# Layer 0 of a hybrid decoder step: convolution products of tile 3 ahead of the last tile 2 unit, tile 2's squares on two engines, the sample tile's squares in their own room

## The chip, the cores and the metric

The kernel runs on all 8 cores of one Trainium2 chip; every core works on one prompt sequence and on 16 of the 128 sample rows, with all the weights. The metric is the device time of the slowest core in microseconds (us). The fast runs of one kernel agreed within 0.2% here. Other runs were in a slower state, in which the cores of one or both dies were granted a lower TensorE clock: in the run of after that took 2964.3 us those of die 1 had 0.899 to 0.908 and those of die 0 0.998 to 0.999.

Engines: PE is TensorE, DVE is VectorE, ACT is ScalarE, POOL is GpSimd, SP is SyncE (here it issues DMA).

## The reference, cut to what matters

Four layers; the change is in the first third of layer 0 alone.

```python
def trunk(x, pool_prev, conv_prev, ffn_prev, pos0, p):
    for l in range(DEPTH):                        # 4
        h = rmsnorm(x, p['norm1'][l])             # D_MODEL 1024
        z = h @ p['w_in'][l]                      # one projection, 1792 columns
        za, zu, zv, zc = ...                      # A: pooling 256; B: u, v 384 each; C: 768
        a_out, pst = pool_mix(za, ...)            # trailing means over 2, 4, 8, 16 rows
        b_out = spatial_gate(zu, zv, ...)
        c_in = zc[..., :D_C] * jax.nn.sigmoid(zc[..., D_C:])     # "the product"
        c_conv, cst = causal_dwconv(c_in, conv_prev[l], ...)     # 31 taps, depthwise
        c_out = jax.nn.silu(layernorm(c_conv, ...))
        x = x + jnp.concatenate([a_out, b_out, c_out], axis=-1) @ p['w_out'][l]
        ...                                       # gated ConvFFN, 2 x 2816 columns
```

## The kernel before

Each core cuts its columns into tiles: 0 to 3 are 512 prompt positions each, 4 is the 64 sample positions. Layer 0 is written as a list of units, and the order of the list is the order of the instructions on each engine:

- `("sq", t)`: eight squares of tile t (one per 128 rows of x), for the RMSNorm; `"M"`: the matmuls with ones that add them up, followed by the reciprocal root on ACT; `("n", t, ks)`: normalised chunks of tile t on DVE.
- `("a", j, t)`: pooling projection j (two of them); its copy out of PSUM is on ACT. `("D", j, t)` and `("P", j, t)`: the pooling steps of (j, t), on DVE or on POOL.
- `("c", j, t)`: the two projections of convolution group j (three of them), the sigmoid on ACT, the product on DVE; for tiles 3 and 4 also a small copy of the new state ("staging").
- `("ho", j)`, `("hi", j)`: when all tiles of group j have their product it is written to DRAM and read back in another layout ("hop-out" and "hop-in"), from which PE makes the convolution as matmuls ("phase convolution").

```python
            def direct(self, ti, m, eng="act"):          # one square, and its sum matmul
                c0, n = TTS[ti]
                q = self.nb % 8                          # ring of eight square buffers, all tiles
                self.nb += 1
                sq = self.sqb[:, q, 0:n]
                src = X[:, m, c0:c0 + n]
                if eng == "act":
                    S.op("act", lambda e: e.activation(sq, src, AF.Square), reads=[RX[m][ti]], writes=[self.Rsq[q]])
                else:
                    S.op(eng, lambda e: e.tensor_tensor(sq, src, src, ALU.mult), reads=[RX[m][ti]], writes=[self.Rsq[q]])
                # ... def mm(): S.op("pe", matmul(pb, ONES, sq)) ... return mm
# ...
                        elif u == "M":
                            while sqs:
                                sqs.pop(0)()
# ...
                        elif u[0] == "sq":
                            sqs.extend(nrm.direct(u[1], m, "dve" if u[1] == 1 and m % 2 else "act") for m in range(KC))
# ...
                lo, hi = range(4), range(4, 8)
                run(("aa", 0, 0, 1), ("c", 0, 0), "T", ("sq", 1), ("c", 1, 0, ["M", ("n", 1, lo)]), ("n", 1, hi), ("P", 0, 0), "L", ("P", 1, 0),
                    ("sq", 4), ("aa", 1, 0), "M", ("sq", 2), ("n", 4, range(KC)), ("c", 0, 1, ["M", ("n", 2, lo)]), ("P", 0, 1), "B", ("c", 1, 1), ("sq", 3), ("n", 2, hi),
                    ("c", 2, 1), "T", ("a", 0, 2), "M", ("n", 3, lo), ("c", 0, 4), ("a", 0, 4), ("a", 1, 4), ("a", 1, 2), ("n", 3, hi), ("c", 1, 4), ("c", 0, 2), ("P", 0, 2), ("c", 1, 2), ("c", 2, 4), ("D", 0, 4),
                    ("c", 2, 2), ("D", 1, 4), ("c", 0, 3), ("ho", 0), ("hi", 0), ("D", 1, 1), ("P", 1, 2), ("c", 1, 3), ("ho", 1), ("c", 2, 3), ("ho", 2), ("hi", 1),
                    ("a", 0, 3), ("a", 1, 3), "O", ("hi", 2))
```

After this list come twelve phase convolutions, each evacuated by ACT and DVE, with the layer norm's sums ("statistics") between them, and then the v projection. The first matmul of the v projection is the mark that I use for the end of the changed part.

## Time and profile before

| | before |
|---|---|
| three runs, us | 2706.82, 2706.22, 3226.61 (slow state) |
| profiled run, us | 2708.28 (spans of the cores 2700.3 to 2707.2, mean 2704.56) |
| PE busy, slowest core | 2675.6 of 2707.2 us |
| first matmul of the v projection, core 5 / mean of 8 | 121.10 / 120.05 us |

The first line of the page and PE's line of its first part (busy us, share of the span, instructions), slowest core, which was core 5:

```profile
span 2707.2 us, 50040 instructions; the slowest of 8 cores (2700.3 to 2707.2 us)
PE 2675.6 (99%) x15858; PEld 1315.2 (49%) x15858; DVE 1745.4 (64%) x3001; ACT 1448.3 (53%) x2825; POOL 594.3 (22%) x898
```

PE is the bound; a gain can come only from time in which PE waits or runs slowly. PE's timeline on core 5. A row is start, duration, engine, line, operation, count, and in brackets the idle time before it with what ended it. L475 adds up squares, L591 is the projection, L886 the phase convolution:

```profile
43.32 3.62 PE L591 MATMUL ps<-H,wsall 128*128 128x512 bf16 x16
47.19 4.01 PE L475 MATMUL ps<-arena,ones 128*128 128x512 bf16 x8 [0.26 <-ACT arena L467]
51.04 8.17 PE L591 MATMUL ps<-H,wsall 128*128 128x512 bf16 x37
...
68.94 23.07 PE L591 MATMUL ps<-H,wsall 128*128 128x512 bf16 x120 [0.45 <-DVE arena L717]
93.12 0.27 PE L886 MATMUL ps<-arena 128*128 128x256 bf16 x1 [1.12 <-ACT arena L738]
...
103.52 0.34 PE L886 MATMUL ps<-arena 128*128 128x256 bf16 x1 [2.73 <-DMA arena<-hop]
```

Three things are to be seen. The eight sum matmuls at 47.19 take 4.01 us, against 1.9 us for eight such matmuls elsewhere (1.89 at 61.60 on this core). The first convolution waited 1.12 us, and the one at 103.52 waited 2.73 us for a hop-in. The squares of the slow group, ACT's timeline of core 5:

```profile
46.43 4.25 ACT L467 ACTIVATE arena<-X 128x512 bf16<-128x512 f32 x8
```

ACT makes all eight alone and starts late: in the list these squares stand behind other work of ACT (copies, a sigmoid, the sample tile's reciprocal root), since they reuse the eight buffers of the sample tile's squares. The issues of the hops, the timeline of SP on core 5 (`hop<-arena` is a hop-out, `arena<-hop` a hop-in):

```profile
85.37 0.33 SPq L138 DMA_DIRECT2D hop<-arena  x1
...
92.18 0.32 SPq L138 DMA_DIRECT2D hop<-arena  x1
...
93.88 0.32 SPq L138 DMA_DIRECT2D hop<-arena  x1
...
96.43 0.37 SPq L138 DMA_DIRECT2D arena<-hop  x1
```

What follows the 2.73 us wait is seen in the windows of core 5 (columns: window, its length, busy us of PE, PEld, DVE, ACT, POOL, then the granted clock, DMA share and GB/s):

```profile
core 5: us, PE busy (x) PEld busy (x) DVE busy (x) ACT busy (x) POOL busy (x), PEclk, DMA share, GB/s
104.00:108.00 4.00, 4.00 (x36) 3.00 (x35) 1.79 (x4) 1.63 (x4) 1.14 (x3) 0.63 1.01 158
```

PE is fully busy in 104 to 108, but at a granted clock of 0.63. DVE's timeline of core 5 at the end of the row that the order will change (L708 is a product, L911 the first evacuation on DVE):

```profile
90.97 1.07 DVE L708 TENSOR_TENSOR arena<-ps,arena 128x512 bf16<-128x512 f32 x1
...
92.68 1.07 DVE L708 TENSOR_TENSOR arena<-ps,arena 128x512 bf16<-128x512 f32 x1 [0.34 <-issue]
...
94.74 0.30 DVE L911 CAST arena<-arena 128x272 bf16<-128x272 f32 x1 [0.69 <-ACT arena L909]
```

### The profile page before, as it was taken

To read this page: it belongs to the slowest core of one execution; us is meant where nothing else is said; L and a number is where in the kernel's file an instruction comes from. 1 tells how busy PE (TensorE), PEld (TensorE's weight loads), DVE (VectorE), ACT (ScalarE), POOL (GpSimd) and SP (SyncE) were. 2 spreads that over 40 slices of the span, in tenths; PEclk is the share of its full clock that TensorE was granted. 3 is DMA by queue.
4 is the path that set the end of the run, shared out by engine and by line. 5 is a ranking of instruction groups with operands and counts; after the bars stand their busy time and mean duration, and the time that the engine had idled before them with its cause. 6 is when DMAs were issued, how large, how long until landed. Compare 5 with 4: busy or idle time off the path is not lost.

```text
span 2707.2 us, 50040 instructions; the slowest of 8 cores (2700.3 to 2707.2 us)
## 1 busy us (share of the span) xinstructions
PE 2675.6 (99%) x15858; PEld 1315.2 (49%) x15858; DVE 1745.4 (64%) x3001; ACT 1448.3 (53%) x2825; POOL 594.3 (22%) x898
## 2 busy tenths in 40 slices
PE   8999999999999999999999999999999999999998
PEld 3554444444465444444446444444445644444444
DVE  4758656566875765656686675565668677565566
ACT  5456627176364654627536473553753657273575
POOL 4444000003315200000412510000051350000005
PEclk9999999999999999999999999999999999999999
DMA  9643222125253321212426131212243522122113
GB/s 245 128 89 58 37 40 36 32 48 91 50 112 64 57 38 32 44 32 48 82 56 131 39 64 31 46 30 48 38 77 85 122 37 49 32 45 39 32 38 129
DMA packets 83888, 170.99 MB, mean 63 GB/s; under 512 B 11120, under 2 KB 44144, under 8 KB 83568
## 3 DMA queue, kind: packets, MB, share of 16 engines
q0 software_dynamic: 31568, 108.44, 24.3%
q1 hardware_dynamic: 52064, 59.35, 7.6%
q8 instruction: 134, 2.20, 0.3%
q14 instruction: 122, 1.00, 0.1%
HBM read 250.37 MB, written 28.39 MB: 103 GB/s over the span
## 4 chain that ended last, share of the span: by engine, by line
PE 92%; DVE 4%; DMA 1%; issue 1%; ACT 1%; SPq 1%; DVEq 0%; POOL 0%; ACTq 0%; POOLq 0%
PE ps L1192 23%; PE ps L1198 23%; PE ps L1108 17%; PE ps L1270 15%; PE ps L591 4%; PE ps L939 3%; PE ps L1036 3%; PE ps L886 1%; DVE arena L708 1%; PE ps L1022 1%; DVE arena L661 1%; DVE arena L645 1%; PE ps L860 1%; DMA X<-xt 1%; SPq L138 1%
## 5 line engine op out<-in xcount | busy, mean ns | idle before, releaser
L1192 PE MATMUL ps<-H,wsall 128*128 128x512 bf16 (+1 forms) x3520 | 700.2, 342 | 0.0
L1198 PE MATMUL ps<-H,wsall 128*128 128x512 bf16 (+1 forms) x3520 | 700.2, 342 | 0.0
L1212 DVE SCALAR_TENSOR_TENSOR arena<-arena,vt_s 128x512 f32<-128x512 f32 (+1 forms) x440 | 289.5, 658 | 382.7 <-ACT arena L1211 365.3
L1207 ACT COPY arena<-ps 128x512 f32<-128x512 f32 (+1 forms) x440 | 224.0, 509 | 576.2 <-PE ps L1192 576.2
L1108 PE MATMUL ps<-arena,wsall 128*128 128x512 bf16 (+2 forms) x2624 | 463.7, 338 | 1.9 <-issue 1.9
L1198 PEld LDWEIGHTS ps<-H,wsall 128*128 128x128 bf16 x3520 | 302.2, 98 | 332.2
L1192 PEld LDWEIGHTS ps<-H,wsall 128*128 128x128 bf16 x3520 | 302.1, 98 | 332.3
L1270 PE MATMUL ps<-arena,wsall 128*128 128x512 bf16 (+1 forms) x2240 | 401.1, 342 | 0.0
L1211 ACT ACTIVATE arena<-ps,vt_s 128x512 f32<-128x512 f32 (+1 forms) x440 | 309.4, 703 | 66.9 <-ACT arena L1207 4.4
L1108 PEld LDWEIGHTS ps<-arena,wsall 128*128 128x128 bf16 x2624 | 220.6, 98 | 237.0 <-issue 2.3
L418 POOL TENSOR_TENSOR arena<-arena 128x512 f32<-128x512 f32 (+2 forms) x273 | 293.7, 1076 | 157.0 <-ACT arena L412 126.2
L1214 DVE SCALAR_TENSOR_TENSOR arena<-arena,vt_s 128x512 f32<-128x512 f32 (+1 forms) x440 | 289.5, 658 | 47.5 <-DVE arena L1212 2.3
L1273 DVE TENSOR_TENSOR X<-ps,X 128x512 f32<-128x512 f32 (+1 forms) x320 | 184.6, 596 | 197.0 <-PE ps L1270 197.0
L412 ACT ACTIVATE arena<-X 128x512 f32<-128x512 f32 (+1 forms) x312 | 169.1, 552 | 239.4 <-DVE X L1110 197.0
L1270 PEld LDWEIGHTS ps<-arena,wsall 128*128 128x128 bf16 x2240 | 188.4, 98 | 211.4
L1110 DVE TENSOR_TENSOR X<-ps,X 128x512 f32<-128x512 f32 (+2 forms) x328 | 188.2, 585 | 142.0 <-PE ps L1108 131.1
L1225 DVE TENSOR_TENSOR arena<-arena 128x512 bf16<-128x512 bf16 (+1 forms) x440 | 260.6, 593 | 3.0 <-ACT arena L1224 2.7
L1217 ACT CAST arena<-ps 128x512 bf16<-128x512 f32 (+1 forms) x440 | 223.8, 509 | 56.2 <-PE ps L1198 48.7
L1224 ACT ACTIVATE arena<-arena 128x512 f32<-128x512 f32 (+1 forms) x440 | 245.4, 559 | 15.6 <-DVE arena L1214 14.9
L591 PE MATMUL ps<-H,wsall 128*128 128x512 bf16 (+1 forms) x1280 | 234.6, 343 | 6.4 <-DVE H L447 3.9
L1219 POOL COPY arena<-arena 128x2 f32<-128x2 f32 x88 | 18.3, 208 | 984.3 <-ACT arena L1207 984.3
L447 DVE SCALAR_TENSOR_TENSOR H<-X,vt_s,ps 128x512 bf16<-128x512 f32 (+1 forms) x320 | 207.2, 649 | 32.5 <-ACT ps L436 17.2
(117 smaller groups left out, 1866.7 us busy)
## 6 DMA issues: line engine op xcount, KB each, us to landing
wsall<-wup POOLq DMA_DIRECT2D x88, 512.0 KB, 6.2
arena<-bnd POOLq DMA_DIRECT2D x32, 480.0 KB, 14.7
wsall<-wdn POOLq DMA_DIRECT2D x32, 448.0 KB, 5.6
hop<-arena SPq DMA_DIRECT2D x24, 544.0 KB, 4.0
arena<-hop SPq DMA_DIRECT2D x24, 544.0 KB, 4.5
X<-xt SPq DMA_DIRECT2D x8, 1024.0 KB, 11.6
wsall<-wout POOLq DMA_DIRECT2D x16, 512.0 KB, 17.0
wsall<-wdn POOLq DMA_DIRECT2D x16, 512.0 KB, 6.2
```

Of the source, the lines that this page charges most:

```text
L418: S.op("pool", lambda e: e.tensor_tensor(dst, in0, sq, ALU.add), reads=R0 + Rs_, writes=Rd)
L591: S.op("pe", lambda e: e.matmul(pb[:, 0:n], wv[:, k, a:a + 128], H[:, k, c0:c0 + n], start=(k == 0), stop=(k == 7)), reads=[Rw, RH[k][ti]] ...
L1108: S.op("pe", lambda e: e.matmul(pb[:, 0:n], lh, rh, start=(q == 0), stop=(q == len(ops) - 1)), reads=rr, writes=[Rpb], inc=(q == len(ops) ...
L1192: S.op("pe", lambda e: e.matmul(pg[:, 0:n], wv[:, k, 0:128], H[:, k, c0:c0 + n], start=(k == 0), stop=(k == 7)), reads=[Rw, RH[k][ti]], wr ...
L1198: S.op("pe", lambda e: e.matmul(pv[:, 0:n], wv[:, k, 128:256], H[:, k, c0:c0 + n], start=(k == 0), stop=(k == 7)), reads=[Rw, RH[k][ti]], ...
L1207: S.op("act", lambda e: e.copy(G[:, gc:gc + n], pg[:, 0:n]), reads=[Rpg], writes=[gw_])
L1211: S.op("act", lambda e: e.activation(T_, pg[:, 0:n], AF.Identity, bias=fb, scale=w2), reads=[Rpg, Rvt2], writes=[Rtm[q]])
L1212: S.op("dve", lambda e: e.scalar_tensor_tensor(T_, G[:, gc - sh:gc - sh + n], w1, T_, ALU.mult, ALU.add), reads=gr_ + [Rvt2], writes=[Rtm[q]])
L1214: S.op("dve", lambda e: e.scalar_tensor_tensor(T_, G[:, gc - 2 * sh:gc - 2 * sh + n], w0, T_, ALU.mult, ALU.add), reads=gr_ + [Rvt2], writ ...
L1224: S.op("act", lambda e: e.activation(T_, T_, AF.Silu), reads=[Rtm[q]], writes=[Rtm[q]])
L1225: S.op("dve", lambda e: e.tensor_tensor(actb[:, fl, c0:c0 + n], VB_, T_, ALU.mult), reads=[Rvst[q], Rtm[q]], writes=[Rab[fl * 5 + ti]])
L1270: S.op("pe", lambda e: e.matmul(pb[:, 0:n], w[1][:, kk, m2 * 128:(m2 + 1) * 128], actb[:, kk, c0:c0 + n], start=(kk == 0), stop=(kk == nf ...
```

## The change

The intent: tile 2's squares early and on two engines, so that PE doesn't wait for them; and the products of groups 0 and 1 of tile 3 before group 2's tile 2, so that their hops leave early. No work is added. For it to be possible, the sample tile's squares get their own room, as the ring of eight buffers would otherwise tie tile 2's to them.

```diff
             def direct(self, ti, m, eng="act"):
                 c0, n = TTS[ti]
-                q = self.nb % 8
-                self.nb += 1
-                sq = self.sqb[:, q, 0:n]
+                if ti == 4 and self.small:
+                    sq, Rsq = self.ab[0][:, n * m:n * m + n], self.small[m]
+                else:
+                    q = self.nb % 8
+                    self.nb += 1
+                    sq, Rsq = self.sqb[:, q, 0:n], self.Rsq[q]
 ...
                         elif u == "M":
-                            while sqs:
+                            for _ in range(KC):
                                 sqs.pop(0)()
 ...
-                            sqs.extend(nrm.direct(u[1], m, "dve" if u[1] == 1 and m % 2 else "act") for m in range(KC))
+                            sqs.extend(nrm.direct(u[1], m, "dve" if u[1] == 1 and m % 2 or u[1] == 2 and m > 3 else "act") for m in range(KC))
 ...
-                    ("sq", 4), ("aa", 1, 0), "M", ("sq", 2), ("n", 4, range(KC)), ...
+                    ("sq", 4), ("sq", 2), ("aa", 1, 0), "M", ("n", 4, range(KC)), ...
-                    ..., ("c", 1, 2), ("c", 2, 4), ("D", 0, 4),
-                    ("c", 2, 2), ("D", 1, 4), ("c", 0, 3), ("ho", 0), ("hi", 0), ("D", 1, 1), ("P", 1, 2), ("c", 1, 3), ("ho", 1), ("c", 2, 3), ("ho", 2), ("hi", 1),
-                    ("a", 0, 3), ("a", 1, 3), "O", ("hi", 2))
+                    ..., ("c", 1, 2), ("c", 2, 4), ("c", 0, 3), ("ho", 0), ("hi", 0),
+                    ("D", 0, 4), ("c", 1, 3), ("ho", 1), ("hi", 1), ("D", 1, 4), ("P", 1, 2), ("c", 2, 2), ("D", 1, 1), ("c", 2, 3), ("ho", 2), ("a", 0, 3), ("a", 1, 3), "O", ("hi", 2))
```

More of the change, by code (lines that the diff above doesn't have):

```diff
@@ L398, in __init__ @@
                 self.nb = 0
+                self.small = None
                 self.gcol = gcol
@@ L461, in direct @@
                 c0, n = TTS[ti]
-                q = self.nb % 8
-                self.nb += 1
-                sq = self.sqb[:, q, 0:n]
+                if ti == 4 and self.small:
[4 more added lines that the diff above has]
+                    sq, Rsq = self.sqb[:, q, 0:n], self.Rsq[q]
                 src = X[:, m, c0:c0 + n]
                 if eng == "act":
-                    S.op("act", lambda e: e.activation(sq, src, AF.Square), reads=[RX[m][ti]], writes=[self.Rsq[q]])
+                    S.op("act", lambda e: e.activation(sq, src, AF.Square), reads=[RX[m][ti]], writes=[Rsq])
                 else:
-                    S.op(eng, lambda e: e.tensor_tensor(sq, src, src, ALU.mult), reads=[RX[m][ti]], writes=[self.Rsq[q]])
+                    S.op(eng, lambda e: e.tensor_tensor(sq, src, src, ALU.mult), reads=[RX[m][ti]], writes=[Rsq])
                 def mm():
@@ L475, in mm @@
                     S.op("pe", lambda e: e.matmul(pb[:, 0:n], ONES[:], sq, start=(m == 0), stop=(m == KC - 1)),
-                         reads=[self.Rsq[q], Rones], writes=[Rpb])
+                         reads=[Rsq, Rones], writes=[Rpb])
                     if m == KC - 1:
@@ L526, in build_nc @@
         nrm = Norm(NB, VT_N1)
+        nrm.small = AR.carve("sqs", NB, 256, 8)[1]
         tail = None
@@ L796, in build_nc @@
                 run(("aa", 0, 0, 1), ("c", 0, 0), "T", ("sq", 1), ("c", 1, 0, ["M", ("n", 1, lo)]), ("n", 1, hi), ("P", 0, 0), "L", ("P", 1, 0),
-                    ("sq", 4), ("aa", 1, 0), "M", ("sq", 2), ("n", 4, range(KC)), ("c", 0, 1, ["M", ("n", 2, lo)]), ("P", 0, 1), "B", ("c", 1, 1), ("sq", 3), ("n", 2, hi),
-                    ("c", 2, 1), "T", ("a", 0, 2), "M", ("n", 3, lo), ("c", 0, 4), ("a", 0, 4), ("a", 1, 4), ("a", 1, 2), ("n", 3, hi), ("c", 1, 4), ("c", 0, 2), ("P", 0, 2), ("c", 1, 2), ("c", 2, 4), ("D", 0, 4),
-                    ("c", 2, 2), ("D", 1, 4), ("c", 0, 3), ("ho", 0), ("hi", 0), ("D", 1, 1), ("P", 1, 2), ("c", 1, 3), ("ho", 1), ("c", 2, 3), ("ho", 2), ("hi", 1),
-                    ("a", 0, 3), ("a", 1, 3), "O", ("hi", 2))
+                    ("sq", 4), ("sq", 2), ("aa", 1, 0), "M", ("n", 4, range(KC)), ("c", 0, 1, ["M", ("n", 2, lo)]), ("P", 0, 1), "B", ("c", 1, 1), ("sq", 3), ("n", 2, hi),
+                    ("c", 2, 1), "T", ("a", 0, 2), "M", ("n", 3, lo), ("c", 0, 4), ("a", 0, 4), ("a", 1, 4), ("a", 1, 2), ("n", 3, hi), ("c", 1, 4), ("c", 0, 2), ("P", 0, 2), ("c", 1, 2), ("c", 2, 4), ("c", 0, 3), ("ho", 0), ("hi", 0),
+                    ("D", 0, 4), ("c", 1, 3), ("ho", 1), ("hi", 1), ("D", 1, 4), ("P", 1, 2), ("c", 2, 2), ("D", 1, 1), ("c", 2, 3), ("ho", 2), ("a", 0, 3), ("a", 1, 3), "O", ("hi", 2))
                 for j in range(2):
```

## The prediction

> **What bounds it now.** The tensor engine is busy 99% of 2707.2 us (page, part 1). The change touches layer 0 alone, the first 120 us. PE's losses there on the slowest core, core 5 (timeline of PE): (a) eight sum matmuls of tile 2's squares take 47.2 to 51.2, 4.0 us where eight cost 1.7: ACT alone makes the squares, 0.53 us each, from 46.4; (b) 1.4 us in three waits for tile 2's normalised chunks (DVE); (c) 1.1 us before the first phase convolution at 93.1 (hop-in 0 lands at 92.7); (d) 2.7 us at 103.5 for hop-in 1, issued at 96.4 behind hop-out 2, landed 103.4; (e) half-speed matmuls after it (pitch 0.24 instead of 0.13 us; granted clock 0.83 in 100:110). [...] From 121 us on PE hardly waits, so what layer 0 saves reaches the end.
>
> **What changes.** No work is added.
> 1. Tile 2's squares: four on ACT after X's first half lands (38.4), four on DVE (0.64 each, as tile 1's) after the second half (42.6), done about 45.2, before PE finishes the projection at 46.9. (a) shrinks to 1.7: PE gains 2.5 us. (b) stays: DVE still makes the same chunks between two products.
> 2. Tile 3's products of groups 0 and 1 come before group 2's tile 2. Hop-out 0 should issue near 77 (85.4 now), hop-out 1 near 80.5 (92.2), hop-in 1 near 85, landing near 90, needed at 98 to 101. (c) and (d) vanish.
> 3. But DVE then carries D04, product, D14 (4.9), product, D11 (5.6), product in one row. PE ends its projections near 89.4, DVE group 2's last product only near 92.7 (94.0 now). [...] the copy of a13 behind D11, and group 2's bank, hold up the second convolution: about 2 us of new PE waiting. The first evacuation starts 1.7 us sooner than now, not 3.6.
>
> **Sum on core 5:** 1.7 from the earlier start, 3.0 from (d) and (e): 4.7 us. Check: core 7 today has no hop stall (0.2 us) and needs 23.4 us from first evacuation to v projection, core 5 26.4; it ends at 2700.3. By the same count core 0 gains 4.3, core 1 5.0, core 7 0.8. The slowest core falls to about 2702; cores draw together.
>
> **Predicted time** 2702.0 us, eight in ten between 2699.3 and 2704.8. Faster by over 2% 0.01, within 2% 0.97, slower 0.02 (a slow-state median).
>
> **What would show it.** Step 1: tile 2's sum matmuls in about 1.8 us, DVE squares near 42.6 to 45.2, the first 64-wide group 2.6 us earlier. Step 2: hop-in 1 issued before hop-out 2, landing before 93; no wait of PE for a hop. Step 3: a new PE wait of 1.5 to 3 us near 89 to 93 released by DVE (or ACT's copy after D11); v projection near 116.4 on core 5 (121.1 now).
>
> **What would make it wrong.** DVE's pool steps may run at other speeds (POOL runs beside them: one op took 0.45 to 1.2 us), moving step 3 by 2 us either way. The new wait could drop the clock again, 1 to 2 us. Bands 6 and 7, asked for after the fourth convolution, take 8.5 to 11 us and could arrive late. X's halves could land after 43.9 on some core and hold DVE up. Chance waits later (1.9 us of issue and 0.8 us for a weight in layer 2 on core 5) decide which core is slowest.

The sum came to 1.7 + 3.0 = 4.7 us on core 5. The 2 us of new waiting in step 3 was my estimate.

## More of the kernel before

Hop-in 1 is issued only at 96.43. Hop-out 2 stands ahead of it in SP's order, but that is not what holds it: its turn comes when hop-out 1, issued at 92.18, has landed. The chain of work that ended last, core 5 (`--critical`: start, duration, what):

```profile
92.18 4.18 DMA hop<-arena
96.43 6.95 DMA arena<-hop
```

On all eight cores hop-in 1 was issued 0.06 to 0.07 us after hop-out 1 had landed, so what makes it late is group 1's product of tile 3.

## The result, and the profile after

| | before | after |
|---|---|---|
| runs, us | 2706.82, 2706.22, 2708.66, (3226.61 slow) | 2706.07, 2704.9, 2704.14, (2964.3 slow) |
| median of all runs, us | 2707.74 | 2705.49 |
| median of the fast runs, us | 2706.82 | 2704.90 |
| first matmul of the v projection, mean of 8 cores, us | 120.05 | 117.55 |
| mean span of the 8 cores, profiled run, us | 2704.56 | 2703.14 |
| slowest core, profiled run, us | 2707.2 (core 5) | 2705.0 (core 1) |

A ratio is the mean time of one kernel's fast runs over that of the other's fast runs of the same rounds, so not quite the ratio of the medians quoted. Here it is 0.9992, with a 95% interval of 0.9969 to 1.0015: the interval does not exclude that nothing was gained. The median of 2705.49 us lies 0.7 us above the range that I gave, that of the fast runs 0.1 us.

The page of after, its slowest core (core 1):

```profile
span 2705.0 us, 50045 instructions; the slowest of 8 cores (2701.3 to 2705.0 us)
PE 2675.8 (99%) x15858; PEld 1314.8 (49%) x15858; DVE 1748.5 (65%) x3005; ACT 1445.2 (53%) x2821; POOL 592.1 (22%) x898
```

PE's timeline on core 5, as before (L479 sums, L596 projection, L890 convolution, L864 statistics):

```profile
47.32 1.89 PE L479 MATMUL ps<-arena,ones 128*128 128x512 bf16 x8
...
66.94 23.07 PE L596 MATMUL ps<-H,wsall 128*128 128x512 bf16 x120 [0.44 <-DVE arena L722]
89.85 0.27 PE L890 MATMUL ps<-arena 128*128 128x256 bf16 x1
...
93.52 0.27 PE L890 MATMUL ps<-arena 128*128 128x256 bf16 x1 [1.53 <-DVE arena L722]
...
95.24 0.61 PE L864 MATMUL ps<-arena,oneb 128*128 128x272 bf16 x3 [0.73 <-DVE arena L918]
```

The sums at 47.32 take 1.89 us instead of 4.01, and no wait for a hop is left. In their place stand 1.53 us before the second convolution, released by DVE's L722, a staging copy, and 0.73 us before the second to fourth statistics matmuls (0.28 us at this place before), released by DVE's L918. All of PE's waits for that line at the statistics came to 2.6 us on core 5, against 1.2 before (`--waits`, 60 to 125 us). Now DVE's timeline of core 5 (L473 tile 2's squares, L713 products, L666 and L650 pooling steps, L722 staging, L915 evacuation):

```profile
42.37 3.61 DVE L473 TENSOR_TENSOR arena<-X 128x512 bf16<-128x512 f32 x4 [0.85 <-DMA X<-xt]
...
76.38 1.08 DVE L713 TENSOR_TENSOR arena<-ps,arena 128x512 bf16<-128x512 f32 x1 [2.38 <-PE ps L596]
...
77.67 1.18 DVE L666 TENSOR_TENSOR fb<-arena 128x291 f32<-128x291 f32 x1
...
91.34 0.75 DVE L650 SCALAR_TENSOR_TENSOR arena<-arena,cstt 128x512 bf16<-128x512 f32 x1
92.01 1.07 DVE L713 TENSOR_TENSOR arena<-ps,arena 128x512 bf16<-128x512 f32 x1
...
93.67 0.30 DVE L915 CAST arena<-arena 128x272 bf16<-128x272 f32 x1 [0.30 <-ACT arena L913]
```

DVE sat idle 2.38 us until the first product at 76.38, and then worked through products and pooling steps in one row until 93. ACT on core 5 (L471 squares, L617 the copy of the last pooling projection, L913 the first evacuation):

```profile
38.93 2.19 ACT L471 ACTIVATE arena<-X 128x512 bf16<-128x512 f32 x4 [1.94 <-DMA X<-xt]
...
92.18 0.20 ACT L617 COPY arena<-arena 128x15 f32<-128x15 f32 x1 [3.16 <-DVE arena L650]
...
93.09 0.48 ACT L913 ACTIVATE arena<-ps,cvq_s 128x272 f32<-128x272 f32 x1
```

ACT waited 3.16 us for DVE's pooling step D11 (L650, started at 91.34) before the copy at 92.18, and so made the first evacuation only at 93.09, though PE had begun the convolutions at 89.85. The hops, SP's timeline:

```profile
77.60 0.33 SPq L138 DMA_DIRECT2D hop<-arena  x1
...
82.26 0.32 SPq L138 DMA_DIRECT2D hop<-arena  x1
...
87.16 0.37 SPq L138 DMA_DIRECT2D arena<-hop  x1
93.21 0.32 SPq L138 DMA_DIRECT2D hop<-arena  x1
```

Hop-in 1 is issued at 87.16, 9.3 us sooner. On cores 2, 3, 6 and 7 the granted clock fell behind the new wait, as it had behind the hop's wait on core 5 of before; windows of core 3 of after:

```profile
97.00:100.00 3.00, 3.00 (x23) 2.09 (x21) 2.13 (x6) 1.43 (x4) 0.00 (x0) 0.50 0.40 81
```

PE is busy for 3.00 of 3.00 us at a granted clock of 0.50. On core 5 there was no such drop. In the traces' clock records each core's clock changes on a grid of 3.41 us: the drop lasted one such step on cores 2, 6 and 7 and two on core 3. In the step just before it PE was busy for 1.4 to 1.6 us on these four cores; the lowest steps of cores 0, 1, 4 and 5 at this place had 1.8 to 2.1 us, and no drop followed (`--windows`). Counted on this grid from 45 to 125 us in the traces of before and after, all nine drops followed a step in which PE was busy for 20 to 52% of the time; the lowest step with no drop behind it had 51%. More than this count is not shown.

### The profile page after: what moved, and what is told of

It reads as the page before. It is cut to its first block, busy times and chain, and to the rows that moved or that the text cites. A ratio compares the mean times of both kernels' runs of the same rounds, so it can differ in the third digit from the quotient of the medians.

```text
span 2705.0 us, 50045 instructions; the slowest of 8 cores (2701.3 to 2705.0 us)
## 1 busy us (share of the span) xinstructions
PE 2675.8 (99%) x15858; PEld 1314.8 (49%) x15858; DVE 1748.5 (65%) x3005; ACT 1445.2 (53%) x2821; POOL 592.1 (22%) x898
## 4 chain that ended last, share of the span: by engine, by line
PE 94%; DVE 3%; DMA 1%; issue 1%; ACT 1%; SPq 1%; POOL 0%; DVEq 0%; ACTq 0%; POOLq 0%
PE ps L1202 23%; PE ps L1196 23%; PE ps L1112 17%; PE ps L1274 15%; PE ps L596 6%; PE ps L943 3%; PE ps L1040 3%; PE ps L890 1%; PE ps L1026 1%; PE ps L864 1%; SPq L138 1%; DMA X<-win 1%; DMA wsall<-win 1%; DVE arena L713 0%; DVE H L448 0%
## 5 line engine op out<-in xcount | busy, mean ns | idle before, releaser
L596 PE MATMUL ps<-H,wsall 128*128 128x512 bf16 (+1 forms) x1280 | 234.7, 344 | 7.1 <-DVE H L448 4.1
```

The lines of the kernel that those rows point to most:

```text
L596: S.op("pe", lambda e: e.matmul(pb[:, 0:n], wv[:, k, a:a + 128], H[:, k, c0:c0 + n], start=(k == 0), stop=(k == 7)), reads=[Rw, RH[k][ti]] ...
```

## The experiments

My theory, A: the squares bring PE forward and earn what layer 0 gained; the order removes the hop waits, but DVE's row behind it ends no earlier, so that the time it saves turns into a wait for DVE and for ACT's copy. Its rivals are that the order earned the gain, or that both did in equal parts; and, for the new wait, D: it is caused by the pooling step D11 standing ahead of group 2's last product, and moving D11 away would give the time back. All twelve kernels compute what the reference computes, and all gave correct results.

The table gives the marks, in us. "Cores 4-7" is needed for squares, order, fill and late11, whose chip had die 0 throttled in every run (mean granted clock 0.984 to 0.998). In the trace of order that began only after 240 us, so its marks stand for all eight cores; in those of squares (cores 0 and 1), fill and late11 (cores 0 to 3) the clock was 0.81 for 15 us from about 47 to 48 us on, and on cores 6 and 7 of late11 for 4 us.

| kernel | tile 2's sums | first convolution | first DVE evacuation | v projection | v projection, cores 4-7 |
|---|---|---|---|---|---|
| before | 3.63 | 93.64 | 95.25 | 120.05 | 119.56 |
| after | 1.52 | 89.89 | 93.63 | 117.55 | 117.36 |
| again (repeat of after) | 1.51 | 89.77 | 93.64 | 117.35 | 117.03 |
| squares | 1.58 | 91.59 | 93.25 | 118.01 | 117.29 |
| order | 3.63 | 92.52 | 95.73 | 119.11 | 119.39 |
| fill | 1.57 | 90.14 | 92.76 | 116.19 | 115.77 |
| fill_again (repeat of fill) | 1.51 | 90.19 | 92.59 | 116.10 | 116.36 |
| late11 | 1.66 | 90.34 | 95.47 | 119.94 | 119.32 |
| fill_pad | 1.52 | 90.16 | 92.55 | 115.84 | 115.83 |
| before_spin27 (layer 0 as before) | 3.63 | 93.05 | 94.66 | 119.14 | 118.84 |
| before_dve8 (layer 0 as before) | 3.63 | 94.56 | 96.17 | 119.88 | 119.81 |
| spin23 (layer 0 as after) | 1.51 | 90.22 | 93.82 | 117.52 | 117.23 |

(A mark is the mean over cores; the sums are counted from the start of the first matmul to the start of the last, so 3.63 here is the 4.01 of the timeline. The last three rows show what a repeat is worth: a mean of before's layer 0 moves by 0.9 us from run to run, one of after's by 0.2. The cores of one run lie 2 to 8 us apart at this mark.)

### squares: the change of the squares alone

```diff
-  ("c", 2, 4), ("c", 0, 3), ("ho", 0), ("hi", 0), ("D", 0, 4), ("c", 1, 3), ("ho", 1), ("hi", 1), ("D", 1, 4), ...
+  ("c", 2, 4), ("D", 0, 4), ("c", 2, 2), ("D", 1, 4), ("c", 0, 3), ("ho", 0), ("hi", 0), ("D", 1, 1), ...      # as before
```

> The changed kernel with the unit order of before from tile 3 on; only the squares of tile 2 and the sample tile are changed. Theory A (the gain of the squares shifts everything after them, the vector engine's row behind it included): tile 2's eight sum matmuls take about 1.8 us instead of 4.0, every later mark of layer 0 comes 2.3 to 2.6 us sooner, the hop waits stay (PE waits of 1 to 4 us for the hop on most cores), the v projection starts 2.3 us sooner than before in the mean of the cores (about 117.8), time about 2705. Rival B (the squares' gain is swallowed by the hop and only the order counts): the v projection starts less than 0.7 us sooner than before.

On the undisturbed die the v projection came at 117.29, 2.3 us before that of before; its four cores lie far apart, though, from 114.55 to 123.02. The waits for the hops stayed: for hop-in 1 they were 0.40 to 2.75 us on the eight cores, in the mean 1.6, against 0.17 to 2.90 and 1.8 in before. PE's timeline of core 5, where that wait was 0.73 us instead of 2.73:

```profile
89.80 0.27 PE L891 MATMUL ps<-arena 128*128 128x256 bf16 x1 [0.85 <-ACT arena L743]
...
98.22 0.27 PE L891 MATMUL ps<-arena 128*128 128x256 bf16 x1 [0.73 <-DMA arena<-hop]
```

Five rounds: 1.0005 (0.9973 to 1.0037), on a chip with die 0 throttled; the mean span of cores 4 to 7 was 2703.65 us (6 runs) against 2705.33 (10 runs of before). So the squares alone give about what both parts together give at the v projection (117.29 against 117.36; different chips, and a spread that leaves 2 us open). The first evacuation, before the waits for hop-in 1, says the same: 93.25, against 94.7 to 96.2 in before and its two repeats, and 93.6 to 93.8 in after and its repeats.

### order: the change of the order alone

```diff
-  ("c", 2, 4), ("D", 0, 4), ("c", 2, 2), ("D", 1, 4), ("c", 0, 3), ("ho", 0), ("hi", 0), ("D", 1, 1), ("P", 1, 2), ("c", 1, 3), ("ho", 1), ...
+  ("c", 2, 4), ("c", 0, 3), ("ho", 0), ("hi", 0), ("D", 0, 4), ("c", 1, 3), ("ho", 1), ("hi", 1), ("D", 1, 4), ("P", 1, 2), ...     # as after
```

> The kernel before with the changed unit order from tile 3 on; the squares are as before. Theory A: the hop waits vanish, but the vector engine's row D04, product, D14, product, D11, product starts 2.5 us later than in the changed kernel and ends 2.5 us later, so the first evacuation comes at about 96 (94.7 before on core 5) and the v projection starts at about 120.0 in the mean of the cores, that is 0 to 0.5 us sooner than before: the order alone gains next to nothing, time 2706 to 2708. Rival B (the order does the work): the v projection starts 2 us or more sooner than before, time about 2705.

PE's timeline of core 5 of this kernel (L475 sums, L885 convolution):

```profile
49.70 4.01 PE L475 MATMUL ps<-arena,ones 128*128 128x512 bf16 x8 [0.25 <-ACT arena L467]
...
96.69 0.27 PE L885 MATMUL ps<-arena 128*128 128x256 bf16 x1 [0.23 <-DVE arena L717]
```

The sums take 4.01 us as before, and the second convolution waits 0.23 us; no core waits for a hop. But the first evacuation moved from 95.25 to 95.73 (DVE's row ends later). From there to the v projection it took 23.4 us instead of 24.8, so that the v projection came at 119.11 in the mean of eight cores, 0.9 us sooner than before; on cores 4 to 7 at 119.39, only 0.2 us sooner than before's 119.56 on another chip. A had expected 0 to 0.5 us, B 2 or more. Time: 0.9999 (0.9954 to 1.0045), three fast runs. At this mark little is gained: most of the wait removed was turned into others, on DVE's row and at the statistics (2.6 us on most cores, as in after).

The end of the program doesn't bear the split out: over the same rounds the mean span of cores 4 to 7 was 2703.63 us in order (3 undisturbed runs), as low as that of squares (2703.65) and 1.7 us under before's 2705.33. The standard error of that difference is about 0.6 us. So how much of the gain is the order's stays open between the 0.2 us of the mark and this; that the hop waits became other waits is what the traces show.

### late11: D11 after group 2's last product

```diff
-  ("D", 1, 4), ("P", 1, 2), ("c", 2, 2), ("D", 1, 1), ("c", 2, 3), ("ho", 2), ("a", 0, 3), ...
+  ("D", 1, 4), ("P", 1, 2), ("c", 2, 2), ("c", 2, 3), ("ho", 2), ("D", 1, 1), ("a", 0, 3), ...
```

> The changed kernel with D11 after group 2's last product and hop-out 2, still ahead of a13. Theory A (the scalar engine's copy of a13 behind D11 holds the first evacuation as much as the bank of group 2 holds the second convolution): the PE wait before the second convolution is gone, hop-out 2 issues about 5 us sooner (88), yet the first evacuation stays within 0.4 us of the changed kernel's (93.7 on core 5), because the copy still waits for D11; the v projection moves by less than 0.7 us. Rival D (the wait that the profile names, the bank of group 2, is the whole cost): the v projection comes 1.5 us or more sooner.

ACT's timeline of core 5 of this kernel:

```profile
94.09 0.20 ACT L617 COPY arena<-arena 128x15 f32<-128x15 f32 x1 [3.64 <-DVE arena L650]
...
95.00 0.48 ACT L913 ACTIVATE arena<-ps,cvq_s 128x272 f32<-128x272 f32 x1
```

And PE's, at the statistics:

```profile
96.21 0.28 PE L864 MATMUL ps<-arena,oneb 128*128 128x272 bf16 x1 [2.13 <-DVE arena L915]
```

The wait before the second convolution vanished, as D said. But the copy at 94.09 waited 3.64 us for D11, which now ended later, the first evacuation on ACT came at 95.00 (93.09 in after), PE waited 2.13 us at the statistics instead (2.1 to 3.6 us on the eight cores, and on seven of them the clock then fell to 0.50), and the v projection came 2.0 us later than after's on the undisturbed die. Rival D falls. Theory A had its direction (no gain) and not its size: I had expected 0.4 to 0.7 us of change, as I hadn't counted that D11 is pushed back by the product now ahead of it.

### fill: two pooling steps earlier, into DVE's idle time

```diff
-  ("c", 2, 4), ("c", 0, 3), ("ho", 0), ("hi", 0), ("D", 0, 4), ("c", 1, 3), ("ho", 1), ("hi", 1), ("D", 1, 4), ("P", 1, 2), ...
+  ("c", 2, 4), ("D", 0, 4), ("c", 0, 3), ("ho", 0), ("hi", 0), ("D", 1, 4), ("c", 1, 3), ("ho", 1), ("hi", 1), ("P", 1, 2), ...
```

> The changed kernel with D04 ahead of group 0's tile 3 product and D14 ahead of group 1's, so that the vector engine works through the 2.4 us in which it waits for that product; nothing else. Theory A (the length of the vector engine's row sets the start of the convolutions): group 2's last product ends near 90.7 to 91.5 instead of 93.1, the PE wait at the second convolution shrinks from 1.5 to under 0.5 us, the first evacuation comes 1.5 to 2.5 us sooner and so does the v projection (mean of the cores about 115.5), time 1.5 to 2.5 us under the changed kernel. Rival C (the evacuation waits for the hop or a13's copy and not for the row): unchanged within 0.5 us.

> The kernel with D04 ahead of group 0's and D14 ahead of group 1's tile 3 product, timed on the same chip as the changed kernel. Theory A: 1 to 2 us faster than the changed kernel, 3.5 to 5 us faster than the kernel before; v projection at about 116.0 in the mean of the cores. Rival: within 0.5 us of the changed kernel.

DVE's timeline of core 5, repeat run on an undisturbed chip:

```profile
74.05 0.45 DVE L666 TENSOR_TENSOR fb<-arena 128x291 f32<-128x291 f32 x1
...
91.02 1.07 DVE L713 TENSOR_TENSOR arena<-ps,arena 128x512 bf16<-128x512 f32 x1
...
92.68 0.30 DVE L915 CAST arena<-arena 128x272 bf16<-128x272 f32 x1 [0.29 <-ACT arena L913]
```

PE's, at the second convolution:

```profile
92.53 0.27 PE L890 MATMUL ps<-arena 128*128 128x256 bf16 x1 [0.41 <-DVE arena L722]
```

D04 now runs at 74.05, where DVE had idled; the last product starts at 91.02 instead of 92.01, the first evacuation at 92.68 instead of 93.67, and PE's wait falls from 1.53 to 0.41 us. The v projection came 1.6 us sooner on cores 4 to 7 in the first run and 1.25 us sooner than `again` in the mean of eight in the second: the direction and, at the low end, the size that A had expected. The first evacuation gained 1.05 us over `again`, less than the 1.5 to 2.5 expected. Time of the second: median 2704.13 us, 0.9988 (0.9976 to 1.0001); `again`, in the same rounds, 2705.56 us, 0.9992 (0.9979 to 1.0006). In the throttled rounds of the first run the interval (0.9979 to 1.0051) tells nothing; the undisturbed die had 2701.21 us (4 runs) against 2705.33 (10 runs of before).

### again, spin23, before_spin27: what comes after layer 0

In the mean, 2.5 us gained at the v projection had become 1.4 us at the end: from v projection to end of span a core took 2584.5 us before and 2585.6 after. I cut that stretch into stages, each bounded by the same two DVE instructions in every kernel (found by counting from the last one) and named by their times in before. Some stages differ between the two kernels by fixed amounts, equal on all eight cores to 0.03 us (one of them to 0.2). Theory T: PE's instruction stream is four records longer, and that shifts something. Two kernels change PE's stream by two matmuls of the warm-up.

```diff
 # spin23, against after
-        spin(25)
+        spin(23)
 # before_spin27, against before
-        spin(25)
+        spin(27)
```

> The changed kernel once more, as the reference on the same chip for the runs beside it and for a second set of eight core traces. Theory A: in the mean of the cores the v projection starts at 117.5 (before 120.05), 2.0 to 3.0 us sooner than before, and the time is 1.5 to 3 us under before, less than the 4.7 us forecast.

> The changed kernel with two of the 25 idle matmuls at its very start left out, so that the tensor engine's whole instruction stream after layer 0 stands four instructions earlier, where it stood in the kernel before (18556 records instead of 18560). Nothing else. Theory T (the 1.1 us that the changed kernel lost after layer 0, in the same places on all eight cores, comes from where its instructions stand in the stream): from v projection to the end it takes 2584.0 to 2584.9 us in the mean of the cores as before (2584.5) instead of 2585.6, and the gaps of 0.4 to 0.6 us at the 12025th, 12368th and 12434th matmul, present on all cores of the changed kernel and on hardly any before, are gone. Rival U (the loss comes from the other engines' streams or from the shifted timing): it stays at 2585.3 to 2586 with those gaps.

> The kernel before with two more idle matmuls at its start: its tensor stream then stands where the changed kernel's stands (18560 records). Theory T: from v projection to end 2585.2 to 2586 us instead of 2584.5, and the changed kernel's gaps at the 12025th, 12368th and 12434th matmul (two places later here) appear on all cores; the marks of layer 0 stay within a us of before. Rival U: the tail stays at 2584 to 2585 with the gaps of before.

The repeat gave 117.35 at the v projection, so layer 0's gain holds. The two spin kernels behaved as their parents in every fixed stage: the stage at 2100 to 2110 us took 11.08 us in before_spin27 as in before, 11.78 in spin23 as in after (11.82). Theory T falls. The whole stretch to the end would not have decided it: it took 2585.1 us in before_spin27 and 2585.2 in spin23, each between the values of the two theories (and 2585.9 in again). Times: 1.0003 (0.999 to 1.0015) for before_spin27 and 0.9991 (0.9979 to 1.0004) for spin23.

One other stage, at 1320 to 1330 us in layer 2, differs from core to core and run to run (10.7 to 13.2 us; in the page of before it is the 1.9 us of "issue" that PE lost on core 5 at L1108). Its mean was 11.42 in before, 12.07 in after, 12.18 in again, 11.51 in spin23, 11.67 in fill_again. It goes with no part of the change that I could name.

### all_act: tile 2's squares early, but all on ACT

```diff
-  "dve" if u[1] == 1 and m % 2 or u[1] == 2 and m > 3 else "act"
+  "dve" if u[1] == 1 and m % 2 else "act"
```

> The kernel after, with all eight squares of tile 2 on ACT again (in their new place ahead of the projection, the sample tile's squares in their own room). It splits the squares change into its two parts. If the place is what gains, ACT makes four squares after X's first half lands and four after the second (42.6 on core 5), 0.53 us each, done near 45, and the eight sum matmuls take 1.5 to 1.9 us as after: the v projection within 0.3 us of after's mean 117.4 to 117.6. If sharing between two engines is what gains, the sums take over 3 us and the v projection comes 1.5 to 2 us later. For what is lost again behind layer 0: DVE's and ACT's streams are nearly those of before, so the stage of layer 2 (2100 to 2110) that took 11.08 us before and 11.8 after on all cores should take 11.1 if it hangs on the length of the instruction streams of the elementwise engines, and 11.8 if not.

Neither expectation for layer 0 was met. ACT's timeline of core 5, the second four squares:

```profile
43.43 2.19 ACT L471 ACTIVATE arena<-X 128x512 bf16<-128x512 f32 x4 [2.45 <-DMA X<-xt]
```

DVE's, the first product behind them:

```profile
47.77 1.08 DVE L713 TENSOR_TENSOR arena<-ps,arena 128x512 bf16<-128x512 f32 x1 [6.29 <-ACT arena L710]
```

PE's, the sums and the last row of projections:

```profile
48.26 1.89 PE L479 MATMUL ps<-arena,ones 128*128 128x512 bf16 x8
...
70.34 1.89 PE L596 MATMUL ps<-H,wsall 128*128 128x512 bf16 x8 [0.44 <-DVE arena L722]
```

The sums take 1.89 us, so the early place is what shortens them. But the second half of x lands late, ACT waits for it (2.45 us) with its copies and sigmoids queued behind, DVE waits 6.29 us for ACT's sigmoid, and everything behind is late: the last row of projections starts at 70.34 (66.94 in after, 68.94 in before). The v projection came at 120.43 on cores 4 to 7, 0.9 us later than before; part of this is a granted clock of 0.50 for 3.4 to 6.8 us from about 61 us, on all four. Sharing the squares with DVE is what keeps ACT's queue moving: the early place on ACT alone doesn't pay. Sharing in the old, late place was not tested. Time: this run's profile fell in the slow state (die 0), so I use cores 4 to 7 alone, which ran at 0.996 to 0.997; two fast runs gave 0.9996 (0.9967 to 1.0025).

For the fixed stages it was decisive. With ACT's and DVE's streams as long as before's, each had before's value: 690 to 720 us took 30.48 on the undisturbed cores, 1450 to 1500 took 50.98, 1800 to 2090 took 290.41 and 2100 to 2110 took 11.08 on three of the four.

### before_dve8, after_act7: longer streams on the elementwise engines

```diff
 # before_dve8, against before
+  for _ in range(8):
+      S.op("dve", lambda e: e.memset(EPST[:, 1:2], 0.0), writes=[Rdum])
 # after_act7, against after
+  for _ in range(7):
+      S.op("act", lambda e: e.activation(EPST[:, 1:2], EPST[:, 0:1], AF.Square), reads=[Rones], writes=[Rdum])
```

> The kernel before with eight writes of one column on DVE at its start, so that DVE's stream is as long as after's (6252 records). Layer 0 as before (v projection 119 to 120 in the mean). If the place of DVE's instructions in their stream makes the fixed shifts of stages in layers 1 and 2, the stage 2100 to 2110 takes 11.8 us on all cores as after; if ACT's or nothing of the kind, 11.08.

> The kernel after with seven one-column squares on ACT at its start, so that ACT's stream is as long as before's (6721 records). Layer 0 as after (v projection 117.4 to 117.6 in the mean). If the place of ACT's instructions in their stream makes the fixed shifts, the stage 2100 to 2110 takes 11.1 us on all cores as before; otherwise 11.8.

Both paddings were longer than meant: each operation waits for the one before it, and a wait is a record of its own. They added 15 and 14 records, not 8 and 7. So the two expected values (11.8 and 11.1 in the stage at 2100) were not met: it was 11.08 and 11.34. The 11.08 is what the first expectation had named for the rival; as the stream was 7 records longer than meant, it decides nothing. But the stages moved, with nothing changed but the length of a stream:

| stage, us from the start | before | all_act | before_dve8 | after_act7 | after | fill_again | fill_pad |
|---|---|---|---|---|---|---|---|
| records DVE / ACT | 6244 / 6721 | 6244 / 6721 | 6259 / 6721 | 6252 / 6728 | 6252 / 6714 | 6251 / 6714 | 6259 / 6721 |
| 690-720 | 30.48 | 30.48 | 30.12 | 30.12 | 30.12 | 30.12 | 30.12 |
| 730-760 | 30.01 | 30.02 | 29.87 | 30.22 | 30.21 | 30.22 | 29.86 |
| 1450-1500 | 50.99 | 50.98 | 51.34 | 51.34 | 51.34 | 51.34 | 51.34 |
| 1800-2090 | 290.41 | 290.40 | 290.07 | 290.35 | 290.63 | 290.35 | 290.05 |
| 2100-2110 | 11.08 | 11.08 | 11.08 | 11.34 | 11.82 | 11.61 | 11.08 |
| 2600-2690 | 89.09 | - | 88.74 | - | 88.99 | 88.74 | 88.74 |

(Medians over unthrottled cores; for after in the stage at 2100 the mean, its cores lie between 11.71 and 11.87. In after_act7 both dies were throttled for parts of the run, at a mean granted clock of 0.953 to 0.967; its values are given for stages in which all its cores agree. Its time is not used.)

This led to the cause. I numbered all records of DVE in a trace from its first, semaphore waits included, and looked at the time from each record to the next. At nearly every record whose number leaves 59 when divided by 128 there is a pause: nine in ten of these gaps are over 0.32 us in every kernel (over 0.38 in before and after), while in any other residue the shortest tenth is about 0.07 us. ACT has the same at the same residue (the shortest tenth from 0.25 to 0.30 us), in every kernel, less sharply in after_act7 (0.09); POOL has one too (0.33 us at residue 64); PE's sequencer shows none. Since the pause falls on the same records on all eight cores (the shortest tenth at this residue is 0.39 us on each core of before and of after), moving it shows as a difference without scatter. Lining up before with before_dve8, where DVE's stream alone differs, nearly all steps of about 0.35 us in DVE's times (493 of 510 on the eight cores, 125 us to the end) lie within a few records of such a record of the one kernel or of the other; with after, where ACT's pauses have moved as well, 485 of 655 do. One of them, DVE's timeline on core 1 of before (L712 and L717 are the sample tile's product and its staging copy):

```profile
711.68 0.23 DVE L712 TENSOR_TENSOR arena<-ps,arena 128x64 bf16<-128x64 f32 x1 [3.53 <-ACT arena L705]
712.38 0.23 DVE L717 TENSOR_TENSOR arena<-ps,arena 128x64 f32<-128x64 f32 x1 [0.47 <-DVE arena L712]
```

The same two operations of after, DVE's timeline on core 1:

```profile
708.28 0.22 DVE L717 TENSOR_TENSOR arena<-ps,arena 128x64 bf16<-128x64 f32 x1 [3.52 <-ACT arena L710]
708.61 0.23 DVE L722 TENSOR_TENSOR arena<-ps,arena 128x64 f32<-128x64 f32 x1
```

In before the semaphore wait between the two rows is DVE's record 1595, which is 12 x 128 + 59, and the second row starts 0.44 us after it; in after the same wait is record 1603, and the row starts 0.07 us after it. The normalised chunks of the next tile stand right behind it, and PE waits for them: this is the 0.36 us by which the stage 690 to 720 is shorter. The change moved four squares from ACT to DVE, which made DVE's stream 8 records longer and ACT's 7 shorter, and so moved every later pause onto other operations, some of which PE waits for. In the fixed stages of after this sums to 0.36 us of loss: -0.35 (130 to 200), -0.36, +0.20, -0.34 (1380 to 1420), +0.35, +0.22, +0.74, -0.10.

What the pause is, is not shown. The page of before lists 122 DMA packets of the kind "instruction" of 8 KB on one queue, as many as there are pauses of DVE and ACT and 128-record steps of POOL and SP on that core (49 + 53 + 18 + 2), and in before and after 99% of the pauses of DVE and ACT are followed by the start of such a packet within 6 us, half of them within 1.3 us; of the records that leave 0 when divided by 128, 10% (before) and 19% (after) are, within 6 us. Why the engine stops at that record stays open.

### fill_pad: the pauses put where they cost less

```diff
 # fill, with eight writes on DVE and seven squares on ACT at the start, each to a column of its own
+  for i in range(8):
+      S.op("dve", lambda e: e.memset(EPST[:, 1 + i:2 + i], 0.0), writes=[Res("pv%d" % i) if i else Rdum])
+  for i in range(7):
+      S.op("act", lambda e: e.activation(EPST[:, 9 + i:10 + i], EPST[:, 0:1], AF.Square), reads=[Rones], writes=[Res("pa%d" % i)])
```

> The kernel fill with eight one-column writes more on DVE and seven one-column squares more on ACT at its start, each without a wait of its own, so one record each: DVE 6251 + 8 = 6259 and ACT 6714 + 7 = 6721 records, the streams of before_dve8. The traces show a pause of about 0.35 us on DVE and on ACT at every 128th record of their streams, and the fixed shifts of stages begin and end at those records. If that is their cause, each fixed stage of fill_pad takes on all cores what it took in before_dve8: 130 to 200 70.57, 690 to 720 30.12, 730 to 760 29.87, 1800 to 2090 290.07 (fill 290.35), 2100 to 2110 11.08 (fill 11.61), 2600 to 2690 88.74; in sum 1.2 us less than fill. The median of fast runs then falls about 1.2 us below fill's 2704.1, to 2703, with chance waits of layer 2 of half a us either way; layer 0's own pauses move too, by up to 0.4 us. If the stages depend on something else, they stay at fill's 290.35 and 11.61 or take other values, and the time stays at fill's.

The streams had 6259 and 6721 records as meant, and the fixed stages took what they had taken in before_dve8, as the table's last column shows (on seven cores of eight in the stage at 2100; the eighth took 11.57). The median was 2703.18 us (six runs, all fast, 2702.56 to 2704.51), 0.9978 (0.9963 to 0.9993) of before: the only kernel whose interval lies below 1. The mean span of all cores fell 4.1 us below before's in the same rounds, against 2.1 us for fill_again in its rounds. The two were not run on the same chip, and the wait in layer 2 was 0.4 us longer in fill_pad's profile; the fixed stages, 1.2 us less in sum than in fill_again, are the part that is shown.

## Why the prediction was right or wrong

**The squares: right.** I had predicted sums of about 1.8 us and a gain of 2.5 us for PE. The sums took 1.89 (four squares took DVE 3.61 us on core 5, not 4 x 0.64, still in time); the last projection matmul came 2.3 us sooner in the mean of eight cores (92.00 to 89.68), and squares alone put the v projection 2.3 us earlier on the undisturbed die.

**The hops: right.** Hop-out 0 near 77 (77.60), hop-out 1 near 80.5 (82.26), hop-in 1 near 85 (87.16) landing near 90 (91.25): no wait of PE for a hop was left. The prediction put hop-in 1's lateness down to hop-out 2 ahead of it; what it waited for was the landing of hop-out 1. The earlier product helps in either case.

**DVE's row turns it into a new wait: right in kind, and nearly in size.** I had predicted about 2 us of new waiting near 89 to 93, released by DVE or by ACT's copy behind D11; it was 1.53 + 0.73 us on core 5, of which 0.28 had been there before. I had expected the first evacuation 1.7 us sooner; it was 1.62 sooner in the mean, 1.07 on core 5, where one pooling unit (D04) took 3.4 us instead of 1.8. POOL worked beside it in both kernels, on different operations; that this is the cause is not shown. That ACT's copy waited for an operation of DVE, and the first evacuation behind it was late, is what the traces show: 3.16 us before the copy in after and 3.64 us in late11; in all_act DVE waited 6.29 us for a sigmoid of ACT, which had itself waited 2.45 us for x. Beyond these waits nothing is shown of how the two engines order their work.

**First failed step: "3.0 from (d) and (e): 4.7 us".** This term was core 5's own, and there it nearly held: from first evacuation to v projection core 5 took 26.4 us before and 23.6 after. But in the mean of the cores it was 24.8 before and 23.9 after, so the term was worth 0.9 us, not 3.0: before, only cores 0, 1 and 5 had run at half the clock behind hop-in 1, and on four cores of after the granted clock was 0.5 for 3.4 us or more behind the new wait, which the prediction had named as a risk (1 to 2 us) and not counted in the sum. Layer 0 gained 2.5 us in the mean (2.7 in the repeat). On the four cores for which I had a figure (0, 1, 5 and 7) I had 3.7 in the mean, and they gained 3.2; singly 6.0, 3.4, 3.8 and -0.6, where I had 4.3, 5.0, 4.7 and 0.8. The span of core 5 did fall by 4.7 us, from 2707.2 to 2702.5, but only 3.8 of it in layer 0: that this figure came out exactly is partly luck.

**Second failed step: "what layer 0 saves reaches the end".** From v projection to the end the mean core took 1.1 us longer than before (repeats of the two differ by 0.3 to 0.7 us among themselves). Shown: 0.36 us of it is the sum of the fixed stages, caused by the pauses at every 128th record, which the moved squares displaced. Argued only: about 0.65 us is the chance wait in layer 2, which other kernels with the same squares (spin23: 11.51, against 11.42 before) didn't have. It stays open what decides that wait.

**Third failed step: "the slowest core falls to about 2702".** The time is the maximum of eight cores, which drew chance waits of PE from 0.3 to 1.9 us each ("issue" and one weight, 125 us to the end, in the profiled runs of before and after; core 7 of before drew none). I took core 5 down by its own losses and forgot that another takes its place: core 1 was the slowest of after, at 2705.0, 1.9 us above the mean of 2703.14. Besides, I gave 2702 for the slowest core's span and for the time, and in both profiled runs the time was 1.07 to 1.08 us above that span (2708.28 and 2707.2, 2706.07 and 2705.0).

**Where the gain of the order went:** it was turned into a new wait on DVE's row and on ACT's copy, and into longer waits for DVE at the statistics. In before PE waited 2.8 us for hops in the mean of the cores; in after it waited for none, but 1.5 us before the second convolution, and 1.3 us more at the statistics (2.5 for 1.3). At the v projection the order alone gave 0.2 us, the squares alone 2.3, both 2.2 (cores 4 to 7; in the mean of eight 0.9, 2.0 and 2.5), figures that repeats of before move by up to 0.9 us; by the spans of the same rounds order and squares gained alike (1.7). With two pooling steps moved into DVE's idle 2.4 us (fill) the v projection came another 1.2 to 1.6 us sooner.

## What to carry to other kernels

When one wait is removed, look up what the next operation behind it waits for, and when that engine's row of work ends: here an order that removed every wait for a hop (2.8 us in the mean) brought the next stage forward by 0.2 to 0.9 us alone, and by 1.2 to 1.6 us more once DVE's idle time ahead of its row was filled. Work out a gain on all cores, not on the slowest, whose losses are partly chance and of which another takes the place. Where tenths of a per cent count, the number of instructions on an elementwise engine was itself a setting here: padding by 7 to 15 records moved the later pauses, and with them single stages by 0.14 to 0.53 us, and a difference equal on all cores to a few hundredths of a microsecond (30.48 against 30.12 us at 690 to 720) was the sign of it.
